# Column tiles of a decoder layer: two K-tiles at a time as wide, narrow, narrow, wide instead of wide, narrow, wide, narrow

## Chip, cores and metric

The kernel runs on one core of one Trainium2 chip. The metric is the device time of one execution in microseconds (us), the median of several runs; less is better. Three runs of the kernel before gave 1110.34, 1111.18 and 1111.68 us.

## What is computed

One layer of a hybrid decoder over 256 tokens of width 2048, in float32:

```python
h = rms_norm(x, ln_mix_pre)
q, k, v, z, xbc, dt = split(h @ w_in)
mixed = concat([attention(q, k, v, rel_bias), ssd(z, xbc, dt)]) @ w_out
x = x + rms_norm(mixed, ln_mix_post)
h = rms_norm(x, ln_ffn_pre)
gate, up = split(causal_dwconv3(h @ w_ffn_up))
f = (gelu(gate) * up) @ w_ffn_down
return x + rms_norm(f, ln_ffn_post)
```

Most of the work is in four products with weight matrices: w_in (2048 x 5648), w_out (2048 x 2048), w_ffn_up (2048 x 11264) and w_ffn_down (5632 x 2048).

## The kernel before

**Precision.** Each operand of a large product is split into a rounded part ("hi") and the remainder ("lo"), both in fp32r. A product is then hi·hi + lo·hi + hi·lo; lo·lo is left out.

**Weights.** They arrive in units of 128 x 1024 values (512 KB). For each unit SyncE starts a DMA into `raw`, ScalarE rounds it to `whi` (L74) and VectorE forms the remainder `wlo` (L75). There are four buffers of each kind, and three more of `whi` and `wlo` from the second half of the kernel on. `ws.take()` hands over the next unit, and `tick()` starts the fetch of another and issues the small work of earlier stages that is due.

**Two kinds of product.** In row tiles (`rows_part`, L272 to L274) the activations are the stationary operand and the weights stream, 512 columns a matmul; they serve v, z, w_out and w_ffn_down. In **column tiles**, which the change touches, the weights are the stationary operand and the activations stream. They serve q, k, xbc and w_ffn_up. A column tile has 128 output columns and one PSUM bank of 512 float32 a partition: the left half collects (lo of the activations)·(hi of the weights), the right half hi·hi and hi·lo.

**The pair.** For each K-tile (128 of the 2048 inputs) `cols_part` issues two matmuls: a **wide** one (L208) with `whi` as weights, over 512 columns (256 of the activations' lo half, 256 of their hi half, from two places of `hT` or `h2`), and a **narrow** one (L209) with `wlo` as weights, over the 256 hi columns alone, into the right half. Each of them loads its own 128 x 128 weights.

**Loops.** `cols_tile` makes one column tile from two units: 16 K-tiles, each a pair, all into the same bank. `cols_first` makes the first eight column tiles at once, at the kernel's start: for each of 16 units (one K-tile of all eight tiles) it issues eight pairs into eight banks. There are 105 calls of `cols_tile` (4 for xbc, 16 for q and k, 85 for w_ffn_up) with 16 pairs each, and 128 pairs in `cols_first`: 1808 pairs. `cols_tok` (L217, L220) is a special form for three tiles of w_ffn_up, with 256 columns in each matmul; the change leaves it alone.

**Order.** A scheduler places each instruction on its engine in the order of the program, except where an operand would be late: near the start it puts some wide matmuls ahead of narrow ones whose `wlo` is not yet there. `cols_sum` (L225, L226) adds the halves of a finished bank on ScalarE and VectorE; there are four banks for column tiles, and `end[0]` is the matmul after which due work is issued.

Of the kernel before, what the change touches and what calls it, by code (L numbers as in the profile page):

```python
# [21 lines left out]
S = 256  # L22
NT = S // P
KT = D // P
# [93 lines left out]
def decoder_layer(ctx, tc, x, xT, win, wdt, wout, wup, wdown, relb, vec, cols, mconv, fconv,  # L118
                  consts, out):
    nc = tc.nc  # L120
# [18 lines left out]
    def tok(t):  # L139
        return slice(t * P, (t + 1) * P)  # L140
# [60 lines left out]
        nc.scalar.activation(hi, src, AF.Copy, scale=w)  # L201
        nc.vector.scalar_tensor_tensor(lo, src, w, f32(hi), op0=ALU.mult, op1=ALU.subtract)

    def cols_part(ps, w, aT, k, j):

        s = tok(j)
        c = slice(k * S, (k + 1) * S)
        nc.tensor.matmul(ps, w[0][:, s], aT[:, :, c], start=(k == 0), stop=False)  # L208
        end[0] = nc.tensor.matmul(ps[:, S:], w[1][:, s], aT[:, 1, c], start=False,  # L209
                                  stop=(k == KT - 1)).ins  # L210

    def cols_tok(ps, w, aT, k, j, t):

# [14 lines left out]
    pending, end = [], [None]  # L228
# [5 lines left out]
    def tick():  # L234
        ws.tick()
        for p in pending:
            p[0] -= 1
        due = [p for p in pending if p[0] <= 0]
        pending[:] = [p for p in pending if p[0] > 0]
        for _, fn, args in due:  # L240
            with tc.issue_after(end[0]):
                fn(*args)

    def cols_tile(ps, aT):
        for u in range(2):
            w = ws.take()
            for j in range(8):
                cols_part(ps, w, aT, u * 8 + j, j)
            tick()

    def cols_first(pss, aT, after):


        for k in range(KT):
            w = ws.take()
            for i, ps in enumerate(pss):
                cols_part(ps, w, aT, k, i)
            tick()
            after(k)

# [3 lines left out]
    def chunk_psums():  # L264
        return [acc.tile([P, 512], F32, name="pa", tag="a") for _ in range(NT)]
# [78 lines left out]
    with ExitStack() as mctx:  # L344
# [3 lines left out]
        with ExitStack() as actx:  # L348
# [60 lines left out]
            def after(k):  # L409
                if k % 2 == 0 and k < 10:  # L410
                    load_x(6 + k, 2)
                elif k == 5:
                    load_small()
                elif k in (7, 9):
                    load_rows((k - 7) // 2)
                elif k == 13:
                    token_rms()

            pab = [psum("pab")] + [col_psum() for _ in range(4)] + [psum("pab") for _ in range(3)]
            cols_first(pab, hT, after)


            pd = psum("pd")[:, :S]
            for k in range(KT):
                g = k % SIDE * 2 * SH
                nc.tensor.matmul(pd[g:g + 2 * SH], wd[:, k, :], xr[:, k, :], start=(k < SIDE),
                                 stop=(k + SIDE >= KT), tile_position=(0, g))
# [203 lines left out]
            for f in range(4, 8):  # L633
                pa = col_psum()
                cols_tile(pa, hT)
                xsT = ax.tile([P, S], F32, name="xsT", tag="xsT", bufs=4)
                cols_sum(xsT, pa)
                conv_mix(f, xsT, xsT)
                defer(4, x_tokens, f, xsT)
# [71 lines left out]
            def head(h):  # L711
                pq = col_psum()
                cols_tile(pq, hT)
                qT, kT = (ax.tile([P, S], F32, name=n, tag="qk", bufs=4) for n in ("qT", "kT"))
                cols_sum(kT, pq)
                nc.vector.scalar_tensor_tensor(qT, kT[:, ::-1], QSCALE, rbc[:, ::-1],
                                               op0=ALU.mult, op1=ALU.mult)
                pk = col_psum()
                cols_tile(pk, hT)
                cols_sum(kT, pk)  # L720
                nc.vector.tensor_tensor(kT, kT, rbc, op=ALU.mult)
                defer(2, logits, h, qT, kT)
# [103 lines left out]
        pss = chunk_psums()  # L826
# [171 lines left out]
    for half in range(2):  # L998
        for i in range(half * HALF, (half + 1) * HALF):
            ps = held_up[2 * i:2 * i + 2]  # L1000
# [128 lines left out]
```

## Time and profile before

| what | value |
|---|---|
| median of three runs | 1111.18 us |
| the profiled execution, its own time | 1110.68 us |
| its span, first to last instruction | 1108.6 us |
| TensorE busy with matmuls | 1101.4 us (99%) |
| weight loads (beside the matmuls) | 945.5 us (85%) |
| VectorE, ScalarE | 784.2 us (71%), 593.1 us (53%) |
| mean granted clock of TensorE | 0.998 |

The span is one execution on the chip, and the profiled execution's own time is 2.1 us above it. A busy TensorE says only that some matmul was under way: the matmuls are pipelined, each lasts longer than the distance to the next start, and what counts is that distance. It is read from the timeline, whose starts are given to 10 ns, as the distance between two far rows divided by the number of matmuls between them.

### The profile page before, as it was taken

Reading aid. Unit: us, or ns where it says so; the run is one execution under the profiler, and the core shown is the slowest. Engines: PE = TensorE matmul, PEld = TensorE weight load, DVE = VectorE, ACT = ScalarE, POOL = GpSimd, SP = SyncE. Lnnn points to the kernel's source line nnn. Section 1 sums busy time; section 2 is a strip of 40 time slices with the busy share of each in tenths; the row PEclk is TensorE's granted clock in tenths of the full one; section 3 lists DMA queues with packets and bytes.
Section 4 is the critical chain, followed back from the end, with each engine's and each line's share of the span. In section 5 each row is a group of like instructions: output and inputs, shape, how many; then the busy total and the mean of one; then the engine's idle time right before and its main releaser. Section 6 shows DMA issues by size and latency. Waiting matters only on the chain.

```text
span 1108.6 us, 15791 instructions
## 1 busy us (share of the span) xinstructions
PE 1101.4 (99%) x5888; PEld 945.5 (85%) x5888; DVE 784.2 (71%) x1270; ACT 593.1 (53%) x914; POOL 15.5 (1%) x26
## 2 busy tenths in 40 slices
PE   9999999999999999999999999999999999999997
PEld 7888888888888988888888888888888888888886
DVE  6699976766567799878787644448787878765553
ACT  6667545545454486555555444345555555554441
POOL 0010000000000000000000000000000000000000
PEclk9999999999999999999999999999999999999999
DMA  8858545555587267555555666565655655656552
GB/s 297 298 188 267 179 152 158 184 172 171 203 304 250 88 226 233 191 191 189 188 192 190 189 197 197 190 193 190 190 190 191 190 190 190 190 205 216 197 161 76
DMA packets 61356, 217.58 MB, mean 196 GB/s; under 512 B 7200, under 2 KB 8624, under 8 KB 60384
## 3 DMA queue, kind: packets, MB, share of 16 engines
q1 hardware_dynamic: 59328, 207.64, 57.4%
q0 software_dynamic: 1664, 8.59, 2.2%
q8 instruction: 46, 0.75, 0.3%
q10 hardware_dynamic: 288, 0.35, 0.1%
q14 instruction: 30, 0.25, 0.1%
HBM read 214.44 MB, written 2.11 MB: 195 GB/s over the span
## 4 chain that ended last, share of the span: by engine, by line
PE 98%; DMA 0%; SPq 0%; ACT 0%; DVE 0%; issue 0%; POOLq 0%; ACTq 0%
PE pa L208 36%; PE pa L209 18%; PE pa L274 9%; PE pa L273 9%; PE pa L272 9%; PE ph L272 4%; PE ph L273 4%; PE ph L274 4%; PE pab L208 1%; PE pa L217 1%; PE py L587 1%; PE pab L209 1%; DMA raw<-in_win_dram 0%; PE pa L220 0%; PE pq L217 0%; PE lg L677 0%
## 5 line engine op out<-in xcount | busy, mean ns | idle before, releaser
L75 DVE TENSOR_TENSOR wlo<-raw,whi 128x1024 fp32r<-128x1024 f32 (+2 forms) x389 | 469.8, 1210 | 249.8 <-ACT whi L74 241.7
L74 ACT CAST whi<-raw 128x1024 fp32r<-128x1024 f32 (+2 forms) x389 | 404.0, 1040 | 417.4 <-PE pa L208 194.9
L208 PE MATMUL pa<-h,whi 128*128 128x512 f32 x1360 | 471.7, 394 | 0.0
L209 PE MATMUL pa<-h,wlo 128*128 128x256 f32 x1360 | 379.1, 279 | 0.0
L208 PEld LDWEIGHTS pa<-h,whi 128*128 128x128 f32 x1360 | 255.5, 188 | 57.4
L209 PEld LDWEIGHTS pa<-h,wlo 128*128 128x128 f32 x1360 | 255.3, 188 | 0.0
L208 PE MATMUL pa<-hT,whi 128*128 128x512 f32 x384 | 136.5, 399 | 0.0
L209 PE MATMUL pa<-hT,wlo 128*128 128x256 f32 x384 | 106.5, 279 | 0.0
L208 PEld LDWEIGHTS pa<-hT,whi 128*128 128x128 f32 x384 | 72.5, 189 | 15.6 <-issue 0.2
L945 DVE SCALAR_TENSOR_TENSOR cfc<-cfu,fcv,cfc 128x254 f32<-128x254 f32 (+1 forms) x176 | 83.5, 479 | 1.5
L209 PEld LDWEIGHTS pa<-hT,wlo 128*128 128x128 f32 x384 | 72.1, 189 | 0.5 <-issue 0.2
L272 PE MATMUL pa<-whi,gT 128*128 128x512 f32 x176 | 68.5, 389 | 0.0
L274 PE MATMUL pa<-whi,gT 128*128 128x512 f32 x176 | 68.5, 389 | 0.0
L274 PE MATMUL ph<-whi,gT 128*128 128x512 f32 x176 | 68.5, 389 | 0.0
L272 PE MATMUL ph<-whi,gT 128*128 128x512 f32 x176 | 68.5, 389 | 0.0
L273 PE MATMUL ph<-wlo,gT 128*128 128x512 f32 x176 | 68.5, 389 | 0.0
L273 PE MATMUL pa<-wlo,gT 128*128 128x512 f32 x176 | 68.5, 389 | 0.0
L943 ACT ACTIVATE cfc<-cfu,fcv 128x256 f32<-128x256 f32 x88 | 52.3, 598 | 1.0 <-DVE cfu L942 1.0
L272 PE MATMUL pa<-whi,hT 128*128 128x512 f32 x128 | 51.1, 399 | 0.0
L274 PE MATMUL pa<-whi,hT 128*128 128x512 f32 x128 | 50.8, 397 | 0.0
L273 PE MATMUL pa<-wlo,hT 128*128 128x512 f32 x128 | 50.7, 396 | 0.0
L272 PE MATMUL pa<-whi,mT 128*128 128x512 f32 x128 | 50.3, 393 | 0.0
(230 smaller groups left out, 1132.1 us busy)
## 6 DMA issues: line engine op xcount, KB each, us to landing
raw<-in_wup_dram SPq DMA_DIRECT2D x176, 512.0 KB, 3.7
raw<-in_wdown_dram SPq DMA_DIRECT2D x88, 512.0 KB, 3.6
raw<-in_win_dram SPq DMA_DIRECT2D x85, 512.0 KB, 3.6
raw<-in_wout_dram SPq DMA_DIRECT2D x32, 512.0 KB, 4.0
xsq<-in_x_dram SPq DMA_DIRECT2D x2, 1024.0 KB, 9.4
rows<-acd POOLq DMA_DIRECT2D x4, 512.0 KB, 7.7
xt<-in_x_dram POOLq DMA_DIRECT2D x2, 1024.0 KB, 6.7
xr<-in_xT_dram SPq DMA_DIRECT2D x6, 256.0 KB, 6.3
```

Source lines behind the costliest of these rows:

```text
L74: nc.scalar.copy(hi[:, s], raw[:, s])
L75: return lambda: nc.vector.tensor_tensor(lo[:, s], raw[:, s], f32(hi[:, s]), op=ALU.subtract)
L208: nc.tensor.matmul(ps, w[0][:, s], aT[:, :, c], start=(k == 0), stop=False)
L209: end[0] = nc.tensor.matmul(ps[:, S:], w[1][:, s], aT[:, 1, c], start=False, stop=(k == KT - 1)).ins
L217: nc.tensor.matmul(both, w[0][:, s], aT[:, :, c:c + S][:, :, tok(t)], start=(t == 0 and k == 0), stop=False)
L272: nc.tensor.matmul(ps, a, w[0][:, s], start=(first and j == 0), stop=False)
L273: nc.tensor.matmul(ps, a, w[1][:, s], start=False, stop=False)
L274: end[0] = nc.tensor.matmul(ps, b, w[0][:, s], start=False, stop=(last and j == 1)).ins
L587: nc.tensor.matmul(py[:, i * 64:(i + 1) * 64], rows[:, t, g, i, :], xcs[t, g][:, i * 64:(i + 1) * 64], start=True, stop=True)
L943: nc.scalar.activation(c, u, AF.Identity, scale=wv[:, 2:3], bias=wv[:, 3:4])
L945: nc.vector.scalar_tensor_tensor(c[:, sh:], u[:, :S - sh], wv[:, 2 - sh:3 - sh], c[:, sh:], op0=ALU.mult, op1=ALU.add)
```

## The change

`cols_part` is divided into `wide` and `narrow`, and `cols_pair` issues two pairs as wide, narrow, narrow, wide. In `cols_tile` the two are neighbouring K-tiles of one tile; in `cols_first` they are two tiles of the same K-tile. For the first K-tile of `cols_first`, where the wide matmul has to clear the bank, the alternating order stays, with the two tiles of each couple exchanged. Instructions, operands, DMAs and buffers are the same.

```diff
--- before.py
+++ after.py
@@ -201,13 +201,23 @@
         nc.scalar.activation(hi, src, AF.Copy, scale=w)
         nc.vector.scalar_tensor_tensor(lo, src, w, f32(hi), op0=ALU.mult, op1=ALU.subtract)
 
-    def cols_part(ps, w, aT, k, j):
-
-        s = tok(j)
-        c = slice(k * S, (k + 1) * S)
-        nc.tensor.matmul(ps, w[0][:, s], aT[:, :, c], start=(k == 0), stop=False)
-        end[0] = nc.tensor.matmul(ps[:, S:], w[1][:, s], aT[:, 1, c], start=False,
-                                  stop=(k == KT - 1)).ins
+    def wide(ps, w, aT, k, j, stop=False):
+
+
+        end[0] = nc.tensor.matmul(ps, w[0][:, tok(j)], aT[:, :, k * S:(k + 1) * S],
+                                  start=(k == 0), stop=stop).ins
+
+    def narrow(ps, w, aT, k, j, stop=False):
+
+        end[0] = nc.tensor.matmul(ps[:, S:], w[1][:, tok(j)], aT[:, 1, k * S:(k + 1) * S],
+                                  start=False, stop=stop).ins
+
+    def cols_pair(a, b, last_a, last_b):
+
+        wide(*a)
+        narrow(*a, stop=last_a)
+        narrow(*b)
+        wide(*b, stop=last_b)
 
     def cols_tok(ps, w, aT, k, j, t):
 
@@ -244,8 +254,9 @@
     def cols_tile(ps, aT):
         for u in range(2):
             w = ws.take()
-            for j in range(8):
-                cols_part(ps, w, aT, u * 8 + j, j)
+            for j in range(0, 8, 2):
+                k = u * 8 + j
+                cols_pair((ps, w, aT, k, j), (ps, w, aT, k + 1, j + 1), False, k + 2 == KT)
             tick()
 
     def cols_first(pss, aT, after):
@@ -253,8 +264,15 @@
 
         for k in range(KT):
             w = ws.take()
-            for i, ps in enumerate(pss):
-                cols_part(ps, w, aT, k, i)
+            for i in range(0, len(pss), 2):
+                a, b = ((pss[i + n], w, aT, k, i + n) for n in range(2))
+                if k == 0:
+                    wide(*b)
+                    narrow(*b)
+                    wide(*a)
+                    narrow(*a)
+                else:
+                    cols_pair(a, b, k == KT - 1, k == KT - 1)
             tick()
             after(k)
```

On TensorE, between two column tiles of w_ffn_up in the first half of the FFN (`pa` is the bank, `h2` the activations, `whi` and `wlo` the two parts of a unit), the order before is

```order
L208 MATMUL pa_5517<-h2_3052,whi_5402 128x512
L209 MATMUL pa_5517<-h2_3052,wlo_5403 128x256
L208 MATMUL pa_5517<-h2_3052,whi_5402 128x512
L209 MATMUL pa_5517<-h2_3052,wlo_5403 128x256
L208 MATMUL pa_5582<-h2_3052,whi_5425 128x512
L209 MATMUL pa_5582<-h2_3052,wlo_5426 128x256
L208 MATMUL pa_5582<-h2_3052,whi_5425 128x512
L209 MATMUL pa_5582<-h2_3052,wlo_5426 128x256
```

and now it is

```order
L212 MATMUL pa_5517<-h2_3052,wlo_5403 128x256 x2
L207 MATMUL pa_5517<-h2_3052,whi_5402 128x512 x2
L212 MATMUL pa_5517<-h2_3052,wlo_5403 128x256 x2
L207 MATMUL pa_5517<-h2_3052,whi_5402 128x512
L207 MATMUL pa_5582<-h2_3052,whi_5425 128x512
L212 MATMUL pa_5582<-h2_3052,wlo_5426 128x256 x2
L207 MATMUL pa_5582<-h2_3052,whi_5425 128x512 x2
L212 MATMUL pa_5582<-h2_3052,wlo_5426 128x256 x2
```

Every second pair is turned round, so that two narrow matmuls and, also across units and tiles, two wide ones stand next to each other.

On TensorE in `cols_first`, at the third K-tile (`pab` and `pa` are banks of the eight tiles), the order before is

```order
L208 MATMUL pab_173<-hT_95,whi_124 128x512
L209 MATMUL pab_173<-hT_95,wlo_125 128x256
L208 MATMUL pa_174<-hT_95,whi_124 128x512
L209 MATMUL pa_174<-hT_95,wlo_125 128x256
L208 MATMUL pa_175<-hT_95,whi_124 128x512
L209 MATMUL pa_175<-hT_95,wlo_125 128x256
L208 MATMUL pa_176<-hT_95,whi_124 128x512
L209 MATMUL pa_176<-hT_95,wlo_125 128x256
```

and now it is

```order
L207 MATMUL pab_173<-hT_95,whi_124 128x512
L212 MATMUL pab_173<-hT_95,wlo_125 128x256
L212 MATMUL pa_174<-hT_95,wlo_125 128x256
L207 MATMUL pa_174<-hT_95,whi_124 128x512
L207 MATMUL pa_175<-hT_95,whi_124 128x512
L212 MATMUL pa_175<-hT_95,wlo_125 128x256
L212 MATMUL pa_176<-hT_95,wlo_125 128x256
L207 MATMUL pa_176<-hT_95,whi_124 128x512
```

Here the two matmuls that stand next to each other write different banks; the order of kinds is the same as in `cols_tile`.

## Rows read from the trace of the kernel before

**Rows 1.** Page, parts 1 and 4: TensorE's busy time; the chain that ended last.
```profile
PE 1101.4 (99%) x5888; PEld 945.5 (85%) x5888; DVE 784.2 (71%) x1270; ACT 593.1 (53%) x914; POOL 15.5 (1%) x26
...
PE 98%; DMA 0%; SPq 0%; ACT 0%; DVE 0%; issue 0%; POOLq 0%; ACTq 0%
PE pa L208 36%; PE pa L209 18%; PE pa L274 9%; PE pa L273 9%; PE pa L272 9%; PE ph L272 4%; PE ph L273 4%; PE ph L274 4%; PE pab L208 1%; PE pa L217 1%; PE py L587 1%; PE pab L209 1%; DMA raw<-in_win_dram 0%; PE pa L220 0%; PE pq L217 0%; PE lg L677 0%
```

**Rows 2.** Waits of TensorE: engine, line, what ended them; total us, times, longest.
```profile
PE pa L979 <- ACT diag L977: 1.6, 1, 1.6
PE idle L327 <- DVE zero L324: 1.1, 1, 1.1
PE pab L209 <- DVE wlo L75: 0.2, 1, 0.2
```

**Rows 3.** Windows, one stretch of column tiles: engines' busy us, granted clock, DMA.
```profile
420.00:600.00 180.00, 180.00 (x1041) 158.07 (x1040) 145.24 (x236) 105.99 (x167) 0.00 (x0) 1.00 0.60 198
```

**Rows 4.** Timeline, TensorE, steady column tiles: start us, own us, line, operation.
```profile
500.08 0.39 PE L208 MATMUL pa<-h,whi 128*128 128x512 f32 x1
500.30 0.28 PE L209 MATMUL pa<-h,wlo 128*128 128x256 f32 x1
500.42 0.40 PE L208 MATMUL pa<-h,whi 128*128 128x512 f32 x1
500.65 0.28 PE L209 MATMUL pa<-h,wlo 128*128 128x256 f32 x1
500.77 0.39 PE L208 MATMUL pa<-h,whi 128*128 128x512 f32 x1
...
509.78 0.39 PE L208 MATMUL pa<-h,whi 128*128 128x512 f32 x1
```

**Rows 5.** Timeline, TensorE: six wide, then six narrow matmuls in a row.
```profile
44.82 0.40 PE L208 MATMUL pab<-hT,whi 128*128 128x512 f32 x1
45.06 1.10 PE L208 MATMUL pa<-hT,whi 128*128 128x512 f32 x4
...
46.23 0.28 PE L209 MATMUL pab<-hT,wlo 128*128 128x256 f32 x1
...
46.94 0.39 PE L208 MATMUL pab<-hT,whi 128*128 128x512 f32 x1
```

**Rows 6.** Timeline, TensorE: two wide, two narrow, then alternating pairs.
```profile
17.08 0.39 PE L208 MATMUL pab<-hT,whi 128*128 128x512 f32 x1
17.31 0.40 PE L208 MATMUL pa<-hT,whi 128*128 128x512 f32 x1
17.54 0.28 PE L209 MATMUL pab<-hT,wlo 128*128 128x256 f32 x1
17.66 0.28 PE L209 MATMUL pa<-hT,wlo 128*128 128x256 f32 x1
17.78 0.39 PE L208 MATMUL pa<-hT,whi 128*128 128x512 f32 x1
...
18.48 0.40 PE L208 MATMUL pa<-hT,whi 128*128 128x512 f32 x1
```

**Rows 7.** Timeline, TensorE: 256-column matmuls alone, 22 intervals from first to last.
```profile
376.67 0.28 PE L217 MATMUL pa<-h,whi 128*128 128x256 f32 x1
...
379.28 0.28 PE L217 MATMUL pq<-h,whi 128*128 128x256 f32 x1
```

**Rows 8.** Timeline, TensorE: 512-column matmuls alone, 13 intervals from first to last.
```profile
700.00 0.39 PE L274 MATMUL ph<-whi,gT 128*128 128x512 f32 x1
...
702.94 0.39 PE L272 MATMUL ph<-whi,gT 128*128 128x512 f32 x1
```

**Rows 9.** Page, part 5: weight loads of the FFN's column tiles.
```profile
L208 PEld LDWEIGHTS pa<-h,whi 128*128 128x128 f32 x1360 | 255.5, 188 | 57.4
L209 PEld LDWEIGHTS pa<-h,wlo 128*128 128x128 f32 x1360 | 255.3, 188 | 0.0
```

**Rows 10.** Waits of ScalarE: for the release of a buffer of rounded weights.
```profile
ACT whi L74 <- PE pa L208: 194.9, 164, 2.6
```

## Prediction

> **What bounds the kernel now.** The first view is the page's busy times and, with it, the chain that ended last [rows 1]. TensorE has a matmul under way in 1101.4 of 1108.6 us, and the chain lies on it for 98%; the column tiles' two lines, L208 and L209, hold 36% + 18% (and 1% + 1% for the `pab` banks), over half of the span. The second view is TensorE's own waits [rows 2]: three, 2.9 us together, one of them at the end of the kernel (L979) and two at its start. So no other engine sets the time; the distance from one matmul's start to the next does. The third view, one long stretch of column tiles [rows 3], shows the engine busy for all of 180 us at a granted clock of 1.00, the higher of its two levels (2.4 GHz). There a column lasts 1/2.4 ns: 512 columns are 213.3 ns, 256 are 106.7.
>
> The fourth view is the timeline, where the change must show. In the steady order [rows 4] a wide matmul starts at 500.08 us and the 28th wide one after it at 509.78: 9.70 us for 28 pairs, 346.4 ns a pair. The columns of a pair are 320 ns, so 26.4 ns are something else, 13.2 for each matmul. The reader should also see that pairs are not alike: the wide matmuls' own times alternate between 0.39 and 0.40, and the first two pairs take 0.34 and 0.35. The steady state is a cycle of **two** pairs, a cheap one and a dear one.
>
> **What the change does, part by part.**
>
> 1. *It removes and adds nothing.* There are 1808 pairs, as many loads of weights as before, the same columns. Eight pairs (the first K-tile of `cols_first`) keep the alternating order, so 1800 pairs, or 900 groups of four matmuls, get the new one. The time can change only through the distances between starts, and one nanosecond a pair is 1.8 us of the kernel.
>
> 2. *Which neighbours it makes.* Before, a matmul is followed by one of the other kind. Now, of four, one narrow is followed by a narrow, one wide by a wide, and two by the other kind. The trace has such neighbours, few but in this very product: where `wlo` was late, the scheduler put wide matmuls together and then their narrow ones.
>  - Once as two wide and two narrow [rows 6]: from 17.08 to 17.78, 0.70 us for the four, **350 ns a pair**. The two alternating pairs that follow, 17.78 to 18.48, take 0.70 us as well: the cheap cycle has been lost and comes back only later.
>  - Once as six and six [rows 5]: the wide ones from 44.82 to 46.23, 235 ns each; the narrow ones from 46.23 to 46.94, 118 ns each; together 2.12 us, **353.3 ns a pair**.
>  So neighbours of one kind took 3.6 to 6.9 ns a pair more than the steady cycle's 346.4.
>
> 3. *Both ends of the price.* The dearest row is 353.3: (353.3 - 346.4) x 1800 = +12.4 us. At the other end there is no reason that excludes a gain, since the cheap pair of the present cycle takes 0.34 us [rows 4]: were all pairs like it, (340 - 346.4) x 1800 = -11.5 us. I take 350, from the row whose order is nearest to the new one (two and two, rows 6): (350 - 346.4) x 1800 = **+6.5 us**.
>
> 4. *What should not matter.* The last reader of a unit's `whi` is now its last matmul, no longer the last but one, so that buffer comes free about 0.12 us later, and `wlo` two matmuls earlier. ScalarE does wait for these releases, 194.9 us in all [rows 10], but it is idle 47% of the time [rows 1], a unit lasts 8 x 346.4 ns = 2.8 us, and none of it reaches TensorE, which over the whole kernel waits 0.2 us for split weights [rows 2]. If that cover went, the loss would be at most the 0.12 us for each of the 226 units, 27 us; nothing in the rows speaks for it, and I cost it at nothing. The scheduler also moves some of ScalarE's roundings and VectorE's operations past each other by a place or two in the FFN; VectorE is busy for 145.2 of 180 us there [rows 3], so it has room, and TensorE writes to one of four banks while another is read. SP's and POOL's instructions stand as before. At the kernel's start, where weights are only just in time, I allow half a microsecond either way.
>
> The sum is made against the profiled execution's own time: 1110.7 + 6.5 = 1117.2 us. The median of the runs shown is 0.5 us above that execution, hence **1117.7 us**.
>
> One could hold that the load of the next weights needs the time of the running matmul, so that it matters what runs beside it. The loads take 188 ns each by their rows [rows 9], more than the 0.12 us between a narrow start and the next, and yet 256-column matmuls one after another, each with weights of its own, keep 2.61 us / 22 = 118.6 ns [rows 7]: successive loads overlap, and two narrow ones in succession are no cliff.
>
> **The rivals.**
>
> *No change (a constant for each matmul).* Each matmul may simply cost its columns and some 13 ns for the change of weights, whoever its neighbours are. For it: the pair's 13.2 ns for each of its two [rows 4], the 512-column matmuls of the row tiles with 2.94 us / 13 = 226.2 ns, 12.9 above their columns [rows 8], and the 256-column ones with 118.6 - 106.7 = 11.9 [rows 7]. Against it: rows 5 and 6, where the same matmuls in another order took more, and the cycle of cheap and dear pairs, which a constant does not explain. Its time is the present one, 1111.2 us. The Trainium skill ("TensorE: Matmul & The Clock Gate", section "Back-to-back issue gap") states such a rule: columns over the clock and 2.5 ns, with no regard to neighbours. The trace disagrees with its size (226.2 where an estimate by the rule is 215.8), and whether it agrees in the indifference to order is what this rival says.
>
> *Faster: the new order settles into cheap pairs.* Something carries over from one pair to the next, or the cycle would not be two pairs long; after each disturbance it takes some pairs to settle [rows 6]. Rows 5 and 6 are such disturbances, not a settled state, so the new order, repeated 900 times, may settle into a cycle of its own. The point from which this decides is a pair of 345.2 ns (1.2 ns less, -2.2 us). Halfway to the cheap pair, 343.2 ns, it gives -3.2 x 1800 = -5.8 us, 1105.4; with all pairs cheap, 1099.7. For it: cheap pairs exist, and the turned pair has two narrow matmuls in succession that read one stretch of the activations on into the next. Against it: no row with this order is cheap.
>
> *Slower still: no settling at all.* If the matmuls keep the price of the long runs [rows 5], the result is +12.4 us, 1123.6.
>
> *The order is not carried out.* The scheduler could have undone it. The rows of the program ahead of this text show that it did not; I give this nothing.
>
> **How the numbers follow.** Forecast (350 ns, with a spread from 348 to 352): 0.42. No settling (353.3): 0.11. No change: 0.24. Faster: 0.23. A measurement of this kernel can tell about 0.2%, 2.2 us, from no change; the forecast's own spread starts at +2.9 us, so the chances are slower 0.53, same 0.24, faster 0.23. For 8 in 10 the range leaves out the faster half of the gains (below 1105) and what lies beyond the dearest row with its half microsecond (above 1124): **1105 to 1124 us**. The likeliest case by itself runs from 1114 to 1122.
>
> **What would show it.** In the timeline of the changed kernel, the distance over 28 pairs in the FFN says everything: near 9.80 us (350 ns) the forecast holds, near 9.70 no change, below 9.66 the faster rival, near 9.89 the price of the runs. The wide matmul that follows a wide one, and the narrow that follows a narrow, should be the ones with the longer own times (0.40, and over 0.28). The row tiles and `cols_tok` should keep 226 and 119 ns, TensorE's waits should stay below 4 us and its granted clock at 1.00. The prediction is wrong if the pair stays at 346.4 or falls below it, or if the time moves through a wait on TensorE that rows 2 do not have.

## The result, and the profile after

| | before | after |
|---|---|---|
| median, us | 1111.26 (6 runs) | 1118.61 (6 runs, 1117.8 to 1120.14) |
| the profiled execution, its own time and its span, us | 1110.68; 1108.6 | 1118.53; 1116.6 |
| ratio to before | | 1.007, 95% interval 1.006 to 1.008 |

The change costs 7.35 us by the medians and 7.85 us between the two profiled executions. The forecast was 1117.7 us.

The page of the changed kernel, parts 1 and 4, answers to [rows 1]:

```profile
PE 1109.2 (99%) x5888; PEld 948.7 (85%) x5888; DVE 785.4 (70%) x1270; ACT 593.6 (53%) x914; POOL 15.6 (1%) x26
...
PE 96%; DVE 2%; DMA 1%; issue 0%; ACT 0%; POOL 0%; POOLq 0%; ACTq 0%
```
TensorE's busy time grew by 7.8 us (1109.2 - 1101.4), nearly the whole of the loss, with the same 5888 matmuls. The loads' and the other engines' busy times moved by 3.2 us at most. TensorE's waits answer to [rows 2] (engine, line, what ended them; total us, times, longest):

```profile
PE pa L997 <- ACT diag L995: 1.6, 1, 1.6
PE idle L345 <- DVE zero L342: 1.1, 1, 1.1
PE px L544 <- DVE xsT L520: 0.4, 1, 0.4
```
They sum to 3.1 us against 2.9, so no wait took part. (The chain now shows 96% instead of 98% for TensorE and 2% for VectorE. With so little waited for, I take that as a neighbouring chain of equal length, not as a new bound.) The stretch of column tiles, by windows (busy us and count of TensorE's matmuls, granted clock, DMA share, GB/s), answers to [rows 3]:

```profile
420.00:600.00 180.00, 180.00 (x1027) 1.00 0.62 194
```
The clock is granted in full as before, and in the same 180 us the engine starts 1027 matmuls instead of 1041. The loss is in the distance between starts. The steady column tiles by the timeline (start us, own us, line, operation; the view puts neighbours of one kind together as x2), which answer to [rows 4]:

```profile
499.81 0.62 PE L207 MATMUL pa<-h,whi 128*128 128x512 f32 x2
500.27 0.40 PE L212 MATMUL pa<-h,wlo 128*128 128x256 f32 x2
500.51 0.63 PE L207 MATMUL pa<-h,whi 128*128 128x512 f32 x2
...
509.64 0.63 PE L207 MATMUL pa<-h,whi 128*128 128x512 f32 x2
```
From 499.81 to 509.64 lie 14 groups of four, or 28 pairs: 9.83 us, **351.1 ns a pair** where it was 346.4. The row tiles over `gT` keep their 13 intervals in 2.94 us, as in [rows 8]:

```profile
704.95 0.39 PE L292 MATMUL ph<-whi,gT 128*128 128x512 f32 x1
...
707.89 0.39 PE L290 MATMUL ph<-whi,gT 128*128 128x512 f32 x1
```
Where the loss lies along the kernel can be read from the first row tile after each stage of column tiles. Before (first row tile over `mT`, then over `gT`):

```profile
278.43 0.40 PE L272 MATMUL pa<-whi,mT 128*128 128x512 f32 x1
...
616.56 0.39 PE L272 MATMUL pa<-whi,gT 128*128 128x512 f32 x1
```
After:

```profile
280.42 0.40 PE L290 MATMUL pa<-whi,mT 128*128 128x512 f32 x1
...
621.53 0.39 PE L290 MATMUL pa<-whi,gT 128*128 128x512 f32 x1
```
Up to the first point, which ends the attention stage, 1.99 us are lost, on 440 pairs in the new order; between the two 4.97 - 1.99 = 2.98 us, on 656 pairs; from there to the end 8.0 - 4.97 = 3.0 us by the spans, on 704 pairs. That is 4.5, 4.5 and 4.3 ns a pair: about the same price in each stage. The two later figures, from the halves of the FFN, are the safe ones; the first also holds the kernel's start, whose time seems to move by about a microsecond of itself (e2 below).

### The profile page after: what moved, and what is told of

Same layout as the page of the kernel before. It is cut to its first block, busy times and chain, and to the rows that moved or that the text cites. A ratio compares the mean times of both kernels' runs of the same rounds, so it can differ in the third digit from the quotient of the medians.

```text
span 1116.6 us, 15789 instructions
## 1 busy us (share of the span) xinstructions
PE 1109.2 (99%) x5888; PEld 948.7 (85%) x5888; DVE 785.4 (70%) x1270; ACT 593.6 (53%) x914; POOL 15.6 (1%) x26
## 4 chain that ended last, share of the span: by engine, by line
PE 96%; DVE 2%; DMA 1%; issue 0%; ACT 0%; POOL 0%; POOLq 0%; ACTq 0%
PE pa L207 35%; PE pa L212 18%; PE pa L292 8%; PE pa L290 8%; PE pa L291 8%; PE ph L292 4%; PE ph L291 4%; PE ph L290 4%; PE pab L207 1%; DVE wlo L75 1%; PE pab L212 1%; PE pa L227 1%; DMA rows<-acd 1%; PE py L605 1%; DVE rows L574 0%
## 5 line engine op out<-in xcount | busy, mean ns | idle before, releaser
L207 PE MATMUL pa<-h,whi 128*128 128x512 f32 x1360 | 427.6, 395 | 0.0
L212 PE MATMUL pa<-h,wlo 128*128 128x256 f32 x1360 | 271.2, 281 | 0.0
L207 PEld LDWEIGHTS pa<-h,whi 128*128 128x128 f32 x1360 | 209.9, 189 | 0.0
L207 PE MATMUL pa<-hT,whi 128*128 128x512 f32 x384 | 126.8, 400 | 0.0
L212 PE MATMUL pa<-hT,wlo 128*128 128x256 f32 x384 | 79.5, 281 | 0.0
L235 ACT COPY cfu<-pa 128x256 f32<-128x256 f32 x87 | 32.0, 370 | 70.6 <-PE pa L207 70.6
L207 PEld LDWEIGHTS pa<-hT,whi 128*128 128x128 f32 x384 | 61.3, 190 | 0.9 <-issue 0.4
L236 DVE TENSOR_TENSOR cfu<-pa,cfu 128x256 f32<-128x256 f32 x87 | 36.5, 421 | 35.3 <-ACT cfu L235 35.3
```

Of the source, the lines that this page charges most:

```text
L207: end[0] = nc.tensor.matmul(ps, w[0][:, tok(j)], aT[:, :, k * S:(k + 1) * S], start=(k == 0), stop=stop).ins
L212: end[0] = nc.tensor.matmul(ps[:, S:], w[1][:, tok(j)], aT[:, 1, k * S:(k + 1) * S], start=False, stop=stop).ins
L235: nc.scalar.copy(dst, ps[:, S:])
L236: nc.vector.tensor_tensor(dst, ps[:, :S], dst, op=ALU.add)
```

## The experiments

The prices of pairs in this section are read alike for all kernels: by windows, from 780 to 960 us, two times 180 us divided by the count of matmuls. The count takes in matmuls that cross the edges, so these values are some tenths of a nanosecond, up to 0.9, low, and one matmul more or less is 0.3 ns; by this reading the kernel before has 1040 matmuls and 346.2 ns, the changed one 1027 and 350.5. The expectations use another reading, whose values lie up to 1.1 ns above these (351.5 for the changed kernel; 353.7 and 346.7 in that of v1).

### Which of the two places (e1, e2)

The first kernel makes `cols_first` as before:

```diff
-            for i in range(0, len(pss), 2):
-                a, b = ((pss[i + n], w, aT, k, i + n) for n in range(2))
...
+            for i, ps in enumerate(pss):
+                wide(ps, w, aT, k, i)
+                narrow(ps, w, aT, k, i, stop=(k == KT - 1))
```

> The new order in cols_tile alone (1680 of the 1808 pairs); cols_first keeps wide, narrow, wide, narrow. Theory (neighbours of one kind are dear, the same amount in every pair): the pair in the FFN stays at about 351 ns as in the changed kernel, and the time is 1111.3 + 1680 x 4.5 ns = 1118.8 us, at most 1 us from the changed kernel's. Rival (part of the loss arises at the start, where the weights are only just in time): at least 2 us below the changed kernel.

The second makes `cols_tile` as before:

```diff
-            for j in range(0, 8, 2):
-                k = u * 8 + j
-                cols_pair((ps, w, aT, k, j), (ps, w, aT, k + 1, j + 1), False, k + 2 == KT)
+            for j in range(8):
+                k = u * 8 + j
+                wide(ps, w, aT, k, j)
+                narrow(ps, w, aT, k, j, stop=(k == KT - 1))
```

> The new order in cols_first alone (120 pairs); cols_tile keeps the old order. Theory: 120 x 4.5 ns = +0.5 us against the kernel before, 1111.8 us, and the FFN's pair at 346.5 ns. Rival (loss at the start): +2 us or more.

Measured: 1118.34 us, ratio 1.0068 (1.0053 to 1.0083), with `cols_tile` alone, 1028 matmuls in the window; 1112.47 us, ratio 1.0014 (1.0004 to 1.0024), with `cols_first` alone, 1041 matmuls. The loss is that of `cols_tile`. The second lies 1.6 us above the kernel before as run beside it (1110.83 us), with an interval from 0.4 to 2.7 us and none of it in the FFN, so whether `cols_first` costs the 0.5 us expected or more is not told apart.

### More neighbours of one kind (e3)

```diff
-            for j in range(0, 8, 2):
-                k = u * 8 + j
-                cols_pair((ps, w, aT, k, j), (ps, w, aT, k + 1, j + 1), False, k + 2 == KT)
+            for j in range(8):
+                wide(ps, w, aT, u * 8 + j, j)
+            for j in range(8):
+                narrow(ps, w, aT, u * 8 + j, j, stop=(u == 1 and j == 7))
```

> cols_tile issues the eight wide matmuls of a unit, then its eight narrow ones; cols_first as in the changed kernel. Theory (each neighbour of the same kind costs, so more of them cost more): a pair of about 353 ns, the price of the run of six and six in the kernel before, 1111.3 + 1680 x 6.7 ns + 0.5 = 1123 us. Rival 1 (the loss comes from the changes between the kinds being mirrored, which runs of eight have less often): a pair at or below 346.5 ns, 1112 us or less. Rival 2 (any order but the strict alternation costs the same): 351 ns, 1119 us.

Measured: 1121.42 us, ratio 1.0096 (1.008 to 1.0111), 1025 matmuls and 351.2 ns. The narrow matmuls of one unit in the timeline, and the wide ones after them:

```profile
801.25 1.12 PE L212 MATMUL pa<-h,wlo 128*128 128x256 f32 x8
802.20 1.09 PE L207 MATMUL pa<-h,whi 128*128 128x512 f32 x4
```
The eight narrow ones take 0.95 us, 118.8 ns each. With seven neighbours of its own kind out of eight a pair costs barely more than with one out of two: 0.7 ns on top of the 4.3 that the change costs by the same reading. The time, 2.8 us above the changed kernel, lies between the theory (1123 us) and its second rival (1119 us). It already speaks against one price for each such neighbour: one neighbour in two costs 4.3 ns a pair, and the step to seven in eight 0.7. (Over 1680 pairs 0.7 ns are 1.2 us; the rest of the 2.8 us is not accounted for.)

### Wide matmuls from one place (e4)

```diff
-        end[0] = nc.tensor.matmul(ps, w[0][:, tok(j)], aT[:, :, k * S:(k + 1) * S],
+        end[0] = nc.tensor.matmul(ps, w[0][:, tok(j)], aT[:, 0, (k - k % 2) * S:(k - k % 2 + 2) * S],
```

> The changed kernel with the wide matmul streaming 512 columns from one place (two neighbouring K-tiles of the lo half) instead of 256 from the lo and 256 from the hi half; so the products that need hi activations times hi weights are left out. Theory A (the price is in how the streamed operand hops between the two halves): wide matmuls fall to the 226 ns of the row tiles and the FFN's pair to about 345 ns, time near 1108 us. Theory B (kind of neighbour alone, wherever the columns come from): the pair stays at 351 ns, near 1118.6 us.

Measured: 1119.68 us, ratio 1.008 (1.006 to 1.01), with 3.2 us of it in a wait for the activations near the start that this edit brings with it; 1030 matmuls, 349.5 ns. The two kinds in a stretch of the FFN (line, engine, operation, count, busy us, mean ns of one):

```profile
L207 PE MATMUL pa<-h,whi 128*128 128x512 f32 x58 | 18.2, 395 | 0.0
L212 PE MATMUL pa<-h,wlo 128*128 128x256 f32 x57 | 11.5, 282 | 0.0
```
The wide matmuls keep their 395 ns, as in the changed kernel, although they now stream one contiguous place. In this stretch, then, the hop from the lo to the hi half inside a matmul is not what costs. But earlier in the FFN the same loop of the same kernel runs at another price:

```profile
395.80 0.62 PE L207 MATMUL pa<-h,whi 128*128 128x512 f32 x2
...
407.58 0.62 PE L207 MATMUL pa<-h,whi 128*128 128x512 f32 x2
...
408.50 0.38 PE L184 MATMUL prb<-cst,rsr 128*128 128x128 f32 x2
```
From 395.80 to 407.58 lie 17 groups of four, 34 pairs of 346.5 ns, the price of the kernel before. At 408.50 two small matmuls of other work come in between, and from then on the pair is dear. So e4 does not settle what the hop costs; it is the first sign that one loop can run at two prices, to which u2 and v1 return. The positions of the two streams were the next thing to try.

### The position of the activations (t1 to t4)

In the program as allocated, the weights' buffers start at bytes 32 or 288 modulo 512 of a partition. In the FFN four buffers of the one kind and three of the other take turns, without any effect on the sequence of distances. So I count positions modulo 256; only two of them, 0 and 128, were tried. `h` starts 128 bytes from the weights' position with its lo half; SHIFT = 32 (values) puts the hi half 128 bytes further, at 0. Four kernels set SHIFT to 0, so that both halves stand alike, with a pad behind `h` that keeps all other tiles where they were. In t1 (changed order) and t3 (order before) both halves stand at 128; in t2 and t4 a larger pad ahead of `h` puts both at 0.

```diff
-SHIFT = 32
+SHIFT = 0
...
-    pad(pers, "pad0", 64)
+    pad(pers, "pad0", 96)
...
     hT = normed("hT")
+    pad(pers, "pad1", 32)
```

(That is t2 and t4; t1 and t3 keep `pad0` at 64 and have 64 in `pad1`.)

> The changed order, with the lo and hi halves of the activations 16384 bytes apart instead of 16512 (SHIFT 0 instead of 32), so that both stand 128 bytes off the weights' position, counted modulo 256. Address theory (what costs is a stream and the load beside it standing 128 bytes apart modulo 256; a hop between the halves is a change of that distance): both halves stand badly, the pair stays at 350 ns or above, time 1118 us or more. Rival (only the order of kinds counts): 351.5 ns, 1118.6 us. This run alone does not part them; it is the partner of the next.

> The changed order, SHIFT 0, and the activations moved by 128 bytes, so that both halves stand at a multiple of 256 bytes from the weights' position. Address theory: wide matmuls near 226 ns and narrow ones near 120 as in the row tiles of w_ffn_down and the run of narrow ones, so a pair near 346 ns, and the row tiles over hT fall from 231 to 227 ns a matmul (384 of them, -1.6 us): time about 1110 us. Rival (only the order of kinds counts): the pair stays at 351.5 ns, time 1117 us or more.

> The order before, SHIFT 0, both halves 128 bytes off modulo 256. Address theory: the cheap cycle of two pairs is gone, a pair of 350 ns or more, time 1117 us or more. Rival (only the order of kinds counts): 346.5 ns, 1111 us.

> The order before, SHIFT 0 and the activations moved by 128 bytes. Address theory: a pair near 346 ns without the two-pair cycle (wide 226, narrow 120), the row tiles over hT at 227 ns: about 1109.7 us. Rival (only the order of kinds counts): 346.5 ns in the two-pair cycle, 1111 us.

| lo, hi half | order before | changed order |
|---|---|---|
| 128, 0 (as given) | 1111.26 us, 346.2 ns | 1118.61 us, 350.5 ns |
| 128, 128 (t3, t1) | 1118.34 us, 350.5 ns | 1114.47 us, 347.5 ns |
| 0, 0 (t4, t2) | 1120.30 us, 352.6 ns | 1113.11 us, 347.8 ns |

The ratios are 1.0063 (1.0048 to 1.0078) for t3, 1.0026 (1.0016 to 1.0036) for t1, 1.0082 (1.0065 to 1.0099) for t4 and 1.0016 (1.0007 to 1.0026) for t2. Both theories fall here. The rival that only the order counts is refuted: with SHIFT 0 the wide, narrow, narrow, wide order is the **cheaper** one, by 3.9 and 7.2 us. And my address theory, a price for each matmul from its own distance to the weights, missed t4 by over 6 ns a pair and t1 to the other side; t3 came out as it said, and t2 3 us above it.

The dear value of t4 is that of its FFN, however, and not of its position alone. Over `hT`, which stands where `h` stands, the same order ran cheaply; first the column tiles at 105 us, then those of the FFN:

```profile
105.64 0.39 PE L208 MATMUL pa<-hT,whi 128*128 128x512 f32 x1
...
116.73 0.39 PE L208 MATMUL pa<-hT,whi 128*128 128x512 f32 x1
```
```profile
500.15 0.40 PE L208 MATMUL pa<-h,whi 128*128 128x512 f32 x1
...
511.46 0.40 PE L208 MATMUL pa<-h,whi 128*128 128x512 f32 x1
```
Each is 32 pairs: 346.6 ns a pair (11.09 us) and 353.4 (11.31 us). So the 7.2 us hold for the price that t4's FFN ran at; the 3.9 us between t3 and t1, where no such second price was found, are the safer sign that the position counts.

For the row tiles the theory gave nearly the right size. Over `hT` they use the hi half twice (L272, L273) and the lo half once (L274) as weights; here the three lines in the kernel before,

```profile
L272 PE MATMUL pa<-whi,hT 128*128 128x512 f32 x128 | 51.1, 399 | 0.0
L273 PE MATMUL pa<-wlo,hT 128*128 128x512 f32 x128 | 50.7, 396 | 0.0
L274 PE MATMUL pa<-whi,hT 128*128 128x512 f32 x128 | 50.8, 397 | 0.0
```
and in t4, with both halves at 0:

```profile
L272 PE MATMUL pa<-whi,hT 128*128 128x512 f32 x128 | 51.1, 400 | 0.0
L273 PE MATMUL pa<-wlo,hT 128*128 128x512 f32 x128 | 50.0, 391 | 0.0
L274 PE MATMUL pa<-whi,hT 128*128 128x512 f32 x128 | 50.1, 391 | 0.0
```
The own time of two of them falls by 5 to 6 ns, to the 0.39 us of the row tiles over `gT` [rows 8], and that of the third stays: 3.3 ns a matmul on average, 1.3 us over 384 of them, where 1.6 us had been expected. Here too a matmul's own distance is not all: L273 has the hi half as weights, which stands at 0 in both kernels, and falls nevertheless; what moved there is the lo half, the weights of the next matmul (L274).

### Is it the position of one against the other? (u1 to u3)

The fourth arrangement has the lo half at 0 and the hi half at 128. u1 (changed order) and u2 (order before) reach it by moving the activations; u3 (changed order) leaves them and moves the weights' buffers instead, and with them all tiles allocated behind them.

```diff
-    pad(pers, "pad0", 64)
+    pad(pers, "pad0", 96)
...
     hT = normed("hT")
+    pad(pers, "pad1", 96)
```

(u1, u2. u3 has `pad1` alone, and `pad2` ahead of the later buffers grows from 48 to 144.)

> The changed order with SHIFT 32 as it was, and the activations moved by 128 bytes against the weights: now the lo half stands at a multiple of 256 bytes from the weights' position and the hi half 128 off, the reverse of the changed kernel. Address theory (order and position together set the price): a pair different from 351.5 ns by at least 1 ns, in a cycle of another pattern; which way it does not say. Rival (the order alone, where the halves are 128 bytes apart): 351.5 ns and 1118.6 us.

> The order before with the activations moved by 128 bytes. Address theory: the cheap cycle of two pairs belongs to this order and that position together and is lost, so a pair above 347.5 ns and more than 1113 us. Rival (order alone, where the halves are 128 bytes apart): 346.9 ns, 1111.2 us.

> The changed order; here the weights' buffers are moved by 384 bytes (128 modulo 256, the other way round the same thing) and the activations stay where they were. Address theory (only the position of the stream relative to the weights counts): the same pair as the run with the activations moved, within 0.5 ns, and the same sequence of distances. Rival (the activations' own position, or any other effect of moving tiles): the pair of the changed kernel, 351.5 ns, or some third value.

Measured: 1117.18 us for u1, ratio 1.0058 (1.0042 to 1.0075), 349.2 ns; 1117.91 us for u3, ratio 1.0063 (1.0048 to 1.0078), 349.5 ns. The sequences, u1 first:

```profile
799.91 0.62 PE L207 MATMUL pa<-h,whi 128*128 128x512 f32 x2
800.37 0.40 PE L212 MATMUL pa<-h,wlo 128*128 128x256 f32 x2
800.61 0.62 PE L207 MATMUL pa<-h,whi 128*128 128x512 f32 x2
...
801.31 0.62 PE L207 MATMUL pa<-h,whi 128*128 128x512 f32 x2
```
```profile
799.84 0.62 PE L207 MATMUL pa<-h,whi 128*128 128x512 f32 x2
800.30 0.40 PE L212 MATMUL pa<-h,wlo 128*128 128x256 f32 x2
800.54 0.62 PE L207 MATMUL pa<-h,whi 128*128 128x512 f32 x2
...
801.24 0.62 PE L207 MATMUL pa<-h,whi 128*128 128x512 f32 x2
```
A constant 0.70 us for each four, with the same 0.46 and 0.24 between kinds, in one and the other, where the changed kernel has 0.46 to 0.47 and 0.23 to 0.24 in turn. So it is the position of the streamed operand against the weights (or against what moves with them) that counts, not that of the stream by itself. In u1 the buffers stand in two ways modulo 512, in u3 all in one, so 256 bytes between them made no difference here. The Trainium skill ("TensorE: Matmul & The Clock Gate", section "Step-by-step: what each phase is for") says that the next weights are read through a port of their own, and that loading them takes no read bandwidth from the running matmul. Taken as a rule for the time, that is not what these runs show: with the activations in place, the move of the weights in u3 changed the sequence of distances, and the pair from 350.5 to 349.5 ns. Whether read bandwidth is what is lost, they do not show.

u2 gave 1117.87 us, ratio 1.0065 (1.005 to 1.008), and with it a surprise. Its windows in the first and the second half of the FFN:

```profile
420.00:600.00 180.00, 180.00 (x1021) 1.00 0.61 194
780.00:960.00 180.00, 180.00 (x1040) 1.00 0.59 190
```
That is 352.6 ns a pair in the first half and 346.2 in the second, with one order, one set of tiles and one position. The wide matmuls' group in a stretch of each half (mean ns of one is the last but one number), first half, then second:

```profile
L208 PE MATMUL pa<-h,whi 128*128 128x512 f32 x58 | 20.5, 396 | 0.0
```
```profile
L208 PE MATMUL pa<-h,whi 128*128 128x512 f32 x59 | 20.5, 389 | 0.0
```
They last 396 ns in one half and 389 in the other. One order in one position can run in two ways, as in t4 and e4.

### Can a disturbance switch it? (v1)

The last kernel is u2 with ten short disturbances: in one unit of each of five feature tiles in either half, the first 2, 3, 4, 6 or 8 wide matmuls come ahead of their narrow ones.

```diff
+KICKS = {6: 2, 9: 3, 12: 4, 15: 6, 18: 8}
...
+            n = kick if u == 1 else 0
+            if n:
+                cols_run(ps, w, aT, 8, n, n == 8)
-            for j in range(8):
+            for j in range(n, 8):
                 cols_part(ps, w, aT, u * 8 + j, j)
```

> The kernel of u2 (order before, activations moved by 128 bytes), whose pair takes 353.7 ns through the first half of the FFN and 346.7 through the second, with five disturbances in each half: in one unit of the feature tiles 6, 9, 12, 15 and 18 of the half, the first 2, 3, 4, 6 or 8 wide matmuls come first and then their narrow ones. Theory (one order in one position has more than one settled cycle, and what went before decides in which it runs): after at least one of the ten disturbances the pair stays, for the hundred pairs up to the next one, at another value than before it, in either half. Rival (something else that differs between the halves sets the pair): it goes back to 353.7 ns after each disturbance of the first half and to 346.7 after each of the second.

Measured: 1118.88 us, ratio 1.0064 (1.0042 to 1.0087). The first disturbance, two wide and two narrow at 450.50, in the timeline:

```profile
450.14 0.40 PE L209 MATMUL pa<-h,whi 128*128 128x512 f32 x1
...
450.50 0.63 PE L247 MATMUL pa<-h,whi 128*128 128x512 f32 x2
450.96 0.40 PE L250 MATMUL pa<-h,wlo 128*128 128x256 f32 x2
451.20 0.39 PE L209 MATMUL pa<-h,whi 128*128 128x512 f32 x1
```
Before it every wide matmul lasts 0.40 us; after it, 0.39. Stretches of 30 us between the disturbances, five in each half, by windows:

```profile
420.00:450.00 30.00, 30.00 (x171) 1.00 0.71 230
452.00:482.00 30.00, 30.00 (x175) 1.00 0.58 189
485.00:515.00 30.00, 30.00 (x171) 1.00 0.58 190
519.00:549.00 30.00, 30.00 (x172) 1.00 0.56 188
554.00:584.00 30.00, 30.00 (x172) 1.00 0.57 183
786.00:816.00 30.00, 30.00 (x175) 1.00 0.58 188
819.00:849.00 30.00, 30.00 (x175) 1.00 0.58 185
852.00:882.00 30.00, 30.00 (x172) 1.00 0.56 186
886.00:916.00 30.00, 30.00 (x171) 1.00 0.57 182
921.00:951.00 30.00, 30.00 (x172) 1.00 0.59 189
```
The first stretch lies ahead of the disturbance by two, the second behind it, the third behind the one by three. 171, 175, 171: the pair fell to the cheap value, stayed there for 30 us and went back. In the second half, which enters in the cheap way, the disturbance by two (between 816 and 819) leaves it so (175, 175), and that by three switches it to the dear one (172). After those by four and by six it stays dear, in either half. So in both halves the pair is cheap after the group of two and dear after a longer one. At the 346.4 ns of [rows 4] 30 us hold 173 starts, at the 353.3 of [rows 5] 170; the one or two more are matmuls across the edges. The theory holds: **two settled cycles in one and the same loop, and two matmuls out of turn are enough to go from one to the other.** Its rival, something else that differs between the halves, falls: either price appears in either half.

## Why the prediction was right, and where its reasons were not

**The bound.** Right: TensorE's busy time rose by 7.8 us of 7.85, its waits by 0.2.

**The change adds nothing but distances (step 1).** Right: same counts, and 4.3 to 4.5 ns a pair in each stage.

**The price by neighbours (step 2 and 3).** The term was sized at 350 - 346.4 = 3.6 ns a pair, and 4.7 came out (351.1 - 346.4) by 28 pairs, where starts given to 10 ns leave some tenths open, and 4.3 to 4.5 by the stages. At 4.4 ns 1800 pairs are 7.9 us instead of 6.5, against 7.85 measured. That the chosen row, two and two in a disturbance, came so near is in part luck: 0.70 us for one group, from starts given to 10 ns, is 350 ns only to within 5, more than the term itself, and such a group is a disturbance, not the settled order. The reading of it was wrong: I wrote that neighbours of one kind cost more. e3 has nearly twice as many of them for 0.7 ns more, and in t1 the same neighbours are cheaper than the alternation in t3, by 350.5 - 347.5 = 3.0 ns. What the rows 5 and 6 sampled was the order in this position of the activations against the weights. Had the same program been allocated as in t3 and t1, the same reasoning from neighbours would have had the wrong sign.

**What should not matter (step 4).** Right: no wait appeared for the releases of buffers or the exchanged places on ScalarE and VectorE.

**The rivals.** The constant for each matmul is refuted: with the same instructions a pair took from 346.2 to 352.6 ns by windows. With it falls, for this stream, the indifference to order in the rule of the Trainium skill that was weighed there ("TensorE: Matmul & The Clock Gate", section "Back-to-back issue gap"). That section gives the rule for an isolated matmul, which the prediction left out, and for a stream of loads and matmuls about 131 ns at 512 columns; the 226.2 ns of [rows 8] disagree with that as well. The mechanism of the faster rival, that the order settles into a cycle of its own, was true, only the outcome was not: the change did settle, at 351.1 ns, and not in a cheaper cycle. That this rival could not be excluded was right; v1 shows that such settling exists, and that a short disturbance can decide which cycle it ends in. Whether the changed order also has a cheap cycle at its own position stays open: all its stages ran at about the same price.

**What would show it.** The distance over 28 pairs came out as 9.83 us, next to the 9.80 that was named for the forecast; TensorE's waits (3.1 us), the granted clock (1.00) and the row tiles (2.94 us for 13 intervals) stayed as named. That the second of two neighbours would be the longer one can't be read: the timeline merges such neighbours.

**No better version.** Of the arrangements tried, the order and position of the kernel before are the best. The nearest is t2 with 1113.11 us, whose row tiles over `hT` gain what its column tiles lose only in part. A t4 whose FFN kept the 346.6 ns that its column tiles had at 105 us might be faster than all of them, by an estimated 1.3 us, the gain of its row tiles; that was not run. What in the chip carries the state of a cycle from one pair to the next stays open: the runs show that it exists, that it depends on the order and on whether the halves stand 0 or 128 bytes from the weights, and that history chooses, but not the part that does it.

## What to carry to other kernels

Where each matmul brings its own weights and TensorE is never idle, the distance between starts is not a property of a matmul: it belongs to a settled cycle, set by the order, by the position of the streamed operand against the weights, and by what ran before. So a change of order, or of allocation, is to be measured in its place, as a distance over many matmuls, and the two are to be tuned together; a gain found at one allocation can be a loss at the next. A few rows in which the wanted order already occurs, at the same positions, can give its price, though only roughly, but not its cause.

## What was not expected of the hardware

- The distance of a pair in one unchanged loop had two stable values, 352.6 and 346.2 ns by windows (u2), and a single group of two wide and two narrow matmuls moved it from the dear one to the cheap one, a group of three and three back (v1).
- Moving the weights, and what lies behind them, by 128 bytes modulo 256 had the same effect, to the pattern of starts, as moving the activations (u1, u3: 349.2 and 349.5 ns), while 256 bytes between the buffers had none.
- The sign of the effect of an order turned with the position: 7.35 us for the alternation at SHIFT 32, 3.9 us against it at SHIFT 0 with both halves at 128 (t3, t1).
- One kernel ran one order at one position at 346.6 ns a pair in an early stage and at 353.4 in the FFN (t4), and in another the cheap price ended at two small matmuls of other work (e4).
